# The forward substitution of the RWKV-7 units on VectorE in place of GpSimd

## The chip, the cores and the metric

One core of one Trainium2 chip runs the whole program. Its engines are called by the names of the profile: PE (TensorE, with PEld for its weight loads), DVE (VectorE), ACT (ScalarE), POOL (GpSimd) and SP (SyncE, which only issues transfers here). The metric is the device time in microseconds (us) of one execution; the kernel before has a median of 2439.64 us over 3 runs.

## The reference, cut to what matters

The block handles 2048 tokens of width 1024. A normed input goes through one combined projection; half of its columns feed a retention group (4 heads), half an RWKV-7 group (8 heads of 64). Then come the output projection, a router and a top-2 mixture of 32 experts, and a last norm. The change lies in the RWKV-7 recurrence:

```
def step(state, inp):
    r_t, k_t, v_t, w_t, a_t, b_t = inp
    sa = jnp.einsum('bhvk,bhk->bhv', state, a_t)
    state = state * w_t[:, :, None, :] + sa[..., None] * b_t[:, :, None, :] + v_t[..., None] * k_t[:, :, None, :]
    return state, jnp.einsum('bhvk,bhk->bhv', state, r_t)

_, y = lax.scan(step, jnp.zeros((B, H, N, N), jnp.float32), xs)
```

The kernel works in chunks of 64 tokens. Within a chunk the recurrence becomes a linear system with a unit triangular 64x64 matrix for each head and chunk, and its inverse is what the forward substitution helps to make.

## The kernel before, in words

**Stages.** The first stage (about 1350 us) makes the projections, the retention and the RWKV-7 recurrence in 4 groups (`g`) of 512 tokens; the second the output projection (its matmuls write tiles `acc` from `wo` and `mT`), the residual and the router; the third the experts. The second stage's first matmuls run already while the last units of the first stage are under way.

**Groups.** For a group, `rwkv_proj` and `ret_head` run the projection matmuls on PE, 128x512 each, into PSUM tiles `pj`: 3368 matmuls write `pj` in the program. Each half of a weight block is loaded into `wraw` (L242), split by ACT (L245) and DVE (L246) into a high and a low part in `whl` (3 buffers), and read by 12 matmuls.

**Units.** RWKV-7 works in 16 units (`u`) of 128 tokens. For a unit `rwkv_prep` builds scaled keys and receptances, multiplies them on PE (`pb`), masks the products into `pt` on DVE (L459; 2 buffers) and makes a transposed copy (L463 on PE). The 32x32 diagonal blocks go through DRAM (`nl_d`, L469) and come back as `ln` (L476), 32 systems on 128 partitions with 32 right sides. The substitution has 31 steps of two operations, each of which needs the one before it: a product of a column of `xl` with a row of `ln` into `tm` (L481), and the sum into `xl` (L483), on 128x8 to 128x76 elements. `xl` goes to DRAM (`xl_d`, L485) and comes back as `t1s` and `t2s` and into `inv` (L498 to L503). `ln`, `xl` and `tm` have one buffer each.

**After it.** `rwkv_inv` transposes `t1s` on PE (L506), copies it on DVE (L507) and joins the blocks into the 64x64 inverses. `rwkv_chain` runs the two chunks through the state `sbd`, which goes from unit to unit; it ends with the sums into `yt` (L555). `rwkv_fin` norms and writes the unit's output.

**What sets the order.** The instructions of the first two stages are put in an order by a scheduler with priorities (10000 ahead for prep, inversion and chain, 9000 for `rwkv_fin`, 2000 for the weight split). It fixes the order of every engine when the program is built. On the chip each engine takes its instructions in that order, and an instruction that waits holds up what stands behind it. The third stage has an order written by hand.

Of the kernel before, what the change touches and what calls it, by code (L numbers as in the profile page):

```python
# [14 lines left out]
ALU = mybir.AluOpType  # L15
# [113 lines left out]
def build(tc, A, out, dbg=None, phases=3):  # L129
    nc = tc.nc  # L130
    V, SC, GP, PE, SY = nc.vector, nc.scalar, nc.gpsimd, nc.tensor, nc.sync
# [51 lines left out]
    if True:  # L183
# [195 lines left out]
        def rwkv_prep(u):  # L379
# [93 lines left out]
            xl = rp.tile([128, 8, 32], F32, name="xl")  # L473
# [4 lines left out]
            for t in range(31):  # L478
                n, r = 31 - t, t // 4 + 1
                tv = tm[:, 0:r * n].rearrange("p (s n) -> p s n", n=n)  # L480
                GP.tensor_tensor(tv, xl[:, 0:r, t:t + 1].to_broadcast([128, r, n]),  # L481
                                ln[:, t:t + 1, t + 1:32].to_broadcast([128, r, n]), op=ALU.mult)
                GP.tensor_tensor(xl[:, 0:r, t + 1:32], xl[:, 0:r, t + 1:32], tv, op=ALU.add)  # L483
            for q in range(4):
                SY.dma_start(xl_d[u].rearrange("l (r q) t -> q l r t", q=4)[q], xl[q * 32:(q + 1) * 32])  # L485
            ST[u] = (ar, pt, bkt, uv, bon, wc, lg)
# [162 lines left out]
        for g in range(NG):  # L649
# [7 lines left out]
            for u in range(u0, u0 + 4):  # L657
                with tc.high_priority(offset=PRW):
                    rwkv_prep(u)
                with tc.high_priority(offset=PRC):  # L660
                    rwkv_inv(u)
                if u >= 2:
                    with tc.high_priority(offset=PRF):
                        rwkv_fin(u - 2)
                if u >= 1:
                    with tc.high_priority(offset=PRC):
                        rwkv_chain(u - 1)
# [22 lines left out]
    if True:  # L690
# [167 lines left out]
        t, PEND = 0, []  # L858
# [410 lines left out]
        for NB in FB:  # L1269
            ss = s2.tile([128, NB], F32, name=f"ssf{NB}")  # L1270
            HF = []
            for i in range(NB):
                t = t0 + i
# [6 lines left out]
            for i in range(NB):  # L1280
                t = t0 + i
# [52 lines left out]
```

## Time and profile before

| | |
|---|---|
| median of 3 runs (lowest, highest) | 2439.64 us (2436.16, 2443.72) |
| the profiled execution: its time, its span | 2436.82 us, 2435.1 us |
| PE / DVE / ACT / POOL busy over the span | 91% / 68% / 47% / 47% |
| mean granted TensorE clock, as a share of 2.4 GHz | 0.948 |
| L481 and L483 on POOL | 992 operations, 179.6 and 185.2 us busy |

The span runs from the first to the last instruction of the program; 1.7 us lie around it. "Busy" is the union of an engine's instructions; idle time "before" a group of instructions is put down to what ended it.

### The profile page before, as it was taken

How to read it: one execution, taken by the hardware profiler on the slowest of the kernel's cores; microseconds unless marked ns; L12 is line 12 of the kernel's file. 1: busy time of each engine (PE TensorE's matmuls, PEld its weight loads, DVE VectorE, ACT ScalarE, POOL GpSimd, SP SyncE). 2: the span in 40 equal slices, each digit the busy share in tenths (PEclk: the TensorE clock that was granted, in tenths of full speed). 3: DMA queues.
4: the chain of work that ended last, by engine and by line, in shares of the span. 5: the costliest groups of instructions: out<-in, count | busy, mean ns of one | idle time of the engine just before them, and what ended most of it. 6: DMA issues, size and time to landing. Idle time of an engine off the chain costs nothing. (4 is left out here: it accounts for less than half of the span.)

```text
span 2435.1 us, 36402 instructions
## 1 busy us (share of the span) xinstructions
PE 2212.5 (91%) x11816; PEld 1815.3 (75%) x11817; DVE 1647.5 (68%) x3498; ACT 1135.7 (47%) x1932; POOL 1154.7 (47%) x1530
## 2 busy tenths in 40 slices
PE   5999899998999988999779999699999999899991
PEld 4888778887778877888668888477777777677770
DVE  4477776888667776686765666655555556777775
ACT  4343433534334344343322222356666666577773
POOL 2035444453442475235553233445555555577770
PEclk9998999999999999999869999799999999999995
DMA  6643255433544335433343354468888888899998
GB/s 211 206 151 98 75 174 149 130 104 100 167 122 132 90 96 159 129 102 95 91 118 116 105 197 144 145 225 251 250 250 249 248 251 249 286 387 386 383 358 294
DMA packets 291298, 454.78 MB, mean 187 GB/s; under 512 B 93392, under 2 KB 164496, under 8 KB 291088
## 3 DMA queue, kind: packets, MB, share of 16 engines
q1 hardware_dynamic: 277136, 414.10, 51.1%
q0 software_dynamic: 13824, 37.80, 6.8%
q8 instruction: 94, 1.54, 0.3%
q14 instruction: 100, 0.82, 0.1%
q10 hardware_dynamic: 144, 0.52, 0.1%
HBM read 375.18 MB, written 81.85 MB: 188 GB/s over the span
## 5 line engine op out<-in xcount | busy, mean ns | idle before, releaser
L148 PE MATMUL pj<-nT,whl 128*128 128x512 f32 x2496 | 627.3, 403 | 12.4 <-DVE nT L315 5.3
L148 PEld LDWEIGHTS pj<-nT,whl 128*128 128x128 f32 x2496 | 465.8, 192 | 109.5 <-DVE nT L315 5.8
L148 PE MATMUL acc<-hl,xT 128*128 128x512 f32 (+1 forms) x2048 | 502.8, 400 | 1.7 <-DVE xT L169 1.4
L908 DVE TENSOR_TENSOR hl<-raw,hl 128x1024 fp32r<-128x1024 f32 x259 | 371.0, 1460 | 152.7 <-ACT hl L907 152.6
L908 POOL TENSOR_TENSOR hl<-raw,hl 128x1024 fp32r<-128x1024 f32 x125 | 337.4, 2709 | 252.0 <-ACT hl L907 235.4
L148 PEld LDWEIGHTS acc<-hl,xT 128*128 128x128 f32 (+1 forms) x2048 | 368.4, 182 | 105.5 <-DVE xT L169 1.5
L907 ACT CAST hl<-raw 128x1024 fp32r<-128x1024 f32 x353 | 360.3, 1048 | 75.0 <-DMA raw<-in_wu_dram 37.7
L245 ACT CAST whl<-wraw 128x512 fp32r<-128x512 f32 x248 | 152.5, 618 | 301.5 <-PE pj L148 233.0
L246 DVE TENSOR_TENSOR whl<-wraw,whl 128x512 fp32r<-128x512 f32 x248 | 185.2, 750 | 131.4 <-ACT whl L245 129.8
L148 PE MATMUL acc<-hl,hT 128*128 128x512 f32 (+1 forms) x1024 | 260.0, 404 | 1.0 <-DVEq L1221 1.0
L481 POOL TENSOR_TENSOR tm<-xl,ln 128x60 f32<-128x60 f32 (+24 forms) x496 | 179.6, 362 | 103.8 <-DMA ln<-nl_d 53.6
L148 PEld LDWEIGHTS acc<-hl,hT 128*128 128x128 f32 (+1 forms) x1024 | 183.2, 184 | 50.9 <-DVEq L1221 1.5
L483 POOL TENSOR_TENSOR xl<-xl,tm 128x60 f32<-128x60 f32 (+24 forms) x496 | 185.2, 373 | 36.5
L148 PE MATMUL acc<-wo,mT 128*128 128x512 f32 x768 | 191.6, 402 | 0.0
L148 PEld LDWEIGHTS acc<-wo,mT 128*128 128x128 f32 x768 | 143.1, 191 | 28.8
L494 POOL COPY mbd<-pt 32x128 f32<-32x128 f32 x64 | 20.1, 315 | 226.1 <-DVE pt L459 200.5
L1138 POOL DMA_INDIRECT h_d<-yo,ti x48 | 103.1, 2148 | 46.3 <-DMA h_d<-yo,ti 33.2
L148 PE MATMUL pj<-whl,nT 128*128 128x256 f32 x768 | 117.9, 305 | 0.3 <-ACT whl L245 0.3
L148 PEld LDWEIGHTS pj<-whl,nT 128*128 128x128 f32 x768 | 105.7, 207 | 2.7 <-ACT whl L245 0.5
L459 DVE TENSOR_TENSOR pt<-pb,cst 64x512 f32<-64x512 f32 x128 | 87.9, 687 | 18.6 <-PE pb L148 16.7
L169 DVE TENSOR_TENSOR xT<-tp,xT 128x512 fp32r<-128x512 f32 x80 | 53.7, 686 | 55.9 <-ACT xT L168 53.7
L148 PE MATMUL pb<-ar,bk 64*128 64x128 f32 x512 | 77.8, 299 | 4.6 <-DVE pt L459 3.3
(445 smaller groups left out, 3279.9 us busy)
## 6 DMA issues: line engine op xcount, KB each, us to landing
raw<-in_wg_dram SPq DMA_DIRECT2D x128, 512.0 KB, 4.9
raw<-in_wu_dram SPq DMA_DIRECT2D x128, 512.0 KB, 6.1
raw<-in_wd_dram SPq DMA_DIRECT2D x128, 512.0 KB, 6.5
wraw<-in_win_dram SPq DMA_DIRECT2D x208, 256.0 KB, 3.0
tr<-pf_d SPq DMA_DIRECT2D x80, 256.0 KB, 3.1
pf_d<-ev SPq DMA_DIRECT2D x52, 256.0 KB, 2.9
x<-in_xt_dram SPq DMA_DIRECT2D x32, 256.0 KB, 5.4
pf_d<-x SPq DMA_DIRECT2D x32, 256.0 KB, 4.0
```

Of the source, the lines that this page charges most:

```text
L148: PE.matmul(o, l, r, start=start, stop=stop)
L169: V.tensor_tensor(dst_l, ps, dst_h.bitcast(F32), op=ALU.subtract)
L245: SC.copy(hl[:, 0], raw)
L246: V.tensor_tensor(hl[:, 1], raw, hl[:, 0].bitcast(F32), op=ALU.subtract)
L459: V.tensor_tensor(pt[zs, i:i + 2, :, z ^ h], psp[zs].rearrange("p (f c) x -> p f c x", f=2), maskp[zs, None, None, :].to_broadcast([64, 2, ...
L481: GP.tensor_tensor(tv, xl[:, 0:r, t:t + 1].to_broadcast([128, r, n]), ln[:, t:t + 1, t + 1:32].to_broadcast([128, r, n]), op=ALU.mult)
L483: GP.tensor_tensor(xl[:, 0:r, t + 1:32], xl[:, 0:r, t + 1:32], tv, op=ALU.add)
L494: GP.tensor_copy(mbd[i * 32:(i + 1) * 32, :, i * 32:(i + 1) * 32], pt[i % 2 * 64:i % 2 * 64 + 32, :, i // 2, 0, 32:64])
L907: (SC.copy if hi is SC else hi.tensor_copy)(hl[:, 0], raw)
L908: lo.tensor_tensor(hl[:, 1], raw, hl[:, 0].bitcast(F32), op=ALU.subtract)
L1138: GP.indirect_dma_start(out=h_d, out_offset=bass.IndirectOffsetOnAxis(ap=idx, axis=0), in_=y, in_offset=None, bounds_check=S + 127, comput ...
```

## The change

The two operations of each step are issued to VectorE. Their operands, shapes, buffers and the transfers around them stay. Because the order of all engines is found anew for the changed program, instructions move on every engine in the first two stages; no instruction is added or taken away.

```
             for t in range(31):
                 n, r = 31 - t, t // 4 + 1
                 tv = tm[:, 0:r * n].rearrange("p (s n) -> p s n", n=n)
-                GP.tensor_tensor(tv, xl[:, 0:r, t:t + 1].to_broadcast([128, r, n]),
+                V.tensor_tensor(tv, xl[:, 0:r, t:t + 1].to_broadcast([128, r, n]),
                                 ln[:, t:t + 1, t + 1:32].to_broadcast([128, r, n]), op=ALU.mult)
-                GP.tensor_tensor(xl[:, 0:r, t + 1:32], xl[:, 0:r, t + 1:32], tv, op=ALU.add)
+                V.tensor_tensor(xl[:, 0:r, t + 1:32], xl[:, 0:r, t + 1:32], tv, op=ALU.add)
```

On DVE the first steps of unit 0 now stand as follows (a piece of the difference; `hv`, `rs_y` are a norm's statistics, `qT` and `ev` the rotary embedding of a retention head):

```order
 L413 RECIPROCAL inv_1163<-inv_1163 128x8
+L481 TENSOR_TENSOR tm<-xl,ln 128x31
 L372 TENSOR_REDUCE hv_2448<-pk 128x4
+L483 TENSOR_TENSOR xl<-xl,tm 128x31
 L373 TENSOR_SCALAR hv_2448<-hv_2448 128x4
-L154 TENSOR_SCALAR rs_y_2451<-hv_2448 128x4
+L481 TENSOR_TENSOR tm<-xl,ln 128x30
 L583 TENSOR_TENSOR qT<-pj,cs_t 128x512
 L584 TENSOR_TENSOR ev<-pj,sn_t 64x512
 L585 TENSOR_TENSOR ev<-pj,sn_t 64x512
+L483 TENSOR_TENSOR xl<-xl,tm 128x30
+L154 TENSOR_SCALAR rs_y_2451<-hv_2448 128x4
```

The steps are threaded between other work of DVE. Over the whole program 437 of the 992 stand directly behind another of them, 555 behind something else. From a unit's first L481 to its last L483 there stand 32 to 134 other DVE instructions, 1245 in all 16 units (80, 32, 47 and 73 in the last four).

On PE, this is what stood ahead of the transposition of `t1s` of unit 12 before (`psr`, `psz` are the chain of a unit, `pk` a retention head):

```order
L148 MATMUL pj<-whl,nT_9617 128x256 x3
L148 MATMUL pj<-whl,nT_9621 128x256 x3
L148 MATMUL pj<-whl,nT_9617 128x256 x3
L148 MATMUL pj<-whl,nT_9621 128x256
L148 MATMUL pb<-ar,bk 128x128 x4
L148 MATMUL pk<-qT,kT 128x128 x4
L148 MATMUL pj<-whl,nT_9621 128x256
L506 MATMUL psi<-cst,t1s 128x128
```

And this is what stands there now:

```order
L148 MATMUL pb<-tr,cst 128x512
L443 MATMUL pb<-cst,tr 128x128 x4
L148 MATMUL acc<-wo_12978,mT 128x512 x3
L148 MATMUL acc<-wo_12977,mT 128x512 x6
L148 MATMUL acc<-wo_12976,mT 128x512 x6
L148 MATMUL acc<-wo_12975,mT 128x512
L148 MATMUL psz<-uv,bkt 128x128 x4
L148 MATMUL psr<-uv,pt 64x64 x4
L148 MATMUL acc<-wo_12975,mT 128x512 x5
L148 MATMUL acc<-wo_12982,mT 128x512 x2
L506 MATMUL psi<-cst,t1s 128x128
```

The projections that stood there are all ahead of it now, and matmuls of the output projection have taken their place. Of the 3368 matmuls that write `pj`, 3065 stood ahead of unit 12's last L463 (the end of its prep on PE) and 3352 do now. Ahead of the L506 of unit 15 stood 247 matmuls of the output projection, and stand 312 now. Between the L506 of units 13 and 14 there is now neither a projection nor an output matmul:

```order
L506 MATMUL psi<-cst,t1s 128x128
L148 MATMUL psi<-t1s,mbd 128x32 x4
L148 MATMUL pb<-cst,tr 128x8 x4
L148 MATMUL psi<-t2s,wbd 128x32 x4
L417 MATMUL pb<-cst,tr 128x128 x4
L148 MATMUL psz<-rs__11287,inv_148 128x64 x4
L148 MATMUL psz<-uv,bkt 128x128 x4
L148 MATMUL psz<-uv,pt 64x64 x4
L566 MATMUL psi<-cst,yt 128x128 x4
L148 MATMUL psi<-lg,lw 128x128 x4
```

Of the units' own work nothing has gone from this piece: it is inversion, prep, chain and norm of neighbouring units.

## Rows read from the trace of the kernel before

**Rows 1.** The page's first part: busy time, share of the span, instructions.
```profile
PE 2212.5 (91%) x11816; PEld 1815.3 (75%) x11817; DVE 1647.5 (68%) x3498; ACT 1135.7 (47%) x1932; POOL 1154.7 (47%) x1530
```

**Rows 2.** Busy time by stretch: PE, PEld, DVE, ACT, POOL, clock, DMA.
```profile
167.00:1341.00 1174.00, 1081.47 (x6355) 919.31 (x6354) 846.53 (x1988) 446.52 (x928) 548.37 (x1206) 0.94 0.40 118
...
1560.00:2435.00 875.00, 795.39 (x3656) 611.99 (x3656) 566.88 (x687) 550.63 (x714) 508.65 (x222) 0.96 0.87 289
```

**Rows 3.** The page's groups: the substitution on POOL (count, busy us, mean ns, idle).
```profile
L481 POOL TENSOR_TENSOR tm<-xl,ln 128x60 f32<-128x60 f32 (+24 forms) x496 | 179.6, 362 | 103.8 <-DMA ln<-nl_d 53.6
...
L483 POOL TENSOR_TENSOR xl<-xl,tm 128x60 f32<-128x60 f32 (+24 forms) x496 | 185.2, 373 | 36.5
```

**Rows 4.** Timeline of POOL: first and last steps of units 12 and 15.
```profile
1098.57 0.24 POOL L481 TENSOR_TENSOR tm<-xl,ln 128x31 f32<-128x31 f32 x1
...
1132.31 0.21 POOL L483 TENSOR_TENSOR xl<-xl,tm 128x8 f32<-128x8 f32 x1
...
1315.56 0.24 POOL L481 TENSOR_TENSOR tm<-xl,ln 128x31 f32<-128x31 f32 x1 [6.25 <-DMA ln<-nl_d]
...
1341.01 0.21 POOL L483 TENSOR_TENSOR xl<-xl,tm 128x8 f32<-128x8 f32 x1
```

**Rows 5.** Waits of PE from 167 to 1341 us: us, times, longest.
```profile
PE psi L506 <- DMA t1s<-xl_d: 36.3, 14, 6.0
```

**Rows 6.** Groups by shape on DVE, 0 to 1600 us: small operations.
```profile
L829 DVE TENSOR_TENSOR oh<-oh,ps 128x64 f32<-128x64 f32 x12 | 2.1, 218 | 0.0
...
L804 DVE TENSOR_TENSOR ie<-lg,ge 128x64 f32<-128x64 f32 x6 | 1.5, 242 | 0.1
...
L829 DVE TENSOR_TENSOR oh<-oh,ps 128x32 f32<-128x32 f32 x8 | 1.3, 185 | 0.0
```

**Rows 7.** Timeline of DVE: small operations, independent and dependent.
```profile
1411.56 0.17 DVE L154 TENSOR_SCALAR rs_y<-sv 128x2 int32<-128x2 int32 x1
1411.64 0.16 DVE L156 TENSOR_SCALAR rs_h<-sv 128x2 f32<-128x2 f32 x1
1411.77 0.17 DVE L155 TENSOR_SCALAR rs_y<-rs_y 128x2 int32<-128x2 int32 x1
1411.97 0.16 DVE L158 TENSOR_TENSOR rs_t<-rs_y 128x2 f32<-128x2 f32 x1
1412.16 0.16 DVE L159 TENSOR_TENSOR rs_t<-rs_t,rs_h 128x2 f32<-128x2 f32 x1
```

**Rows 8.** The weight split L246 on DVE: the page's group; its shortest, median, longest.
```profile
L246 DVE TENSOR_TENSOR whl<-wraw,whl 128x512 fp32r<-128x512 f32 x248 | 185.2, 750 | 131.4 <-ACT whl L245 129.8
...
L246 DVE TENSOR_TENSOR whl<-wraw,whl x248: 660/693/1809, 25.6 to 1171.9; 128x512 fp32r<-128x512 f32 x124
```

**Rows 9.** The rotary operation on either engine, first 1400 us.
```profile
L586 POOL TENSOR_TENSOR qT<-qT,ev 128x512 f32<-128x512 f32 x16 | 25.0, 1560 | 24.4 <-DVE ev L585 19.9 <-DMA ev<-in_x_dram 4.5
...
L583 DVE TENSOR_TENSOR qT<-pj,cs_t 128x512 f32<-128x512 f32 x16 | 10.9, 684 | 1.6 <-PE pj L148 1.3
```

**Rows 10.** Waits of DVE from 167 to 1341 us, the longest two.
```profile
DVE whl L246 <- ACT whl L245: 81.2, 72, 3.1
DVE t1s L507 <- PE psi L506: 26.3, 9, 6.6
```

**Rows 11.** Busy time by stretch, as rows 2: DVE's busiest tenth; the units 12 to 15.
```profile
500.00:600.00 100.00, 91.33 (x573) 80.61 (x571) 82.02 (x180) 41.22 (x82) 43.74 (x82) 0.93 0.33 95
...
1099.00:1341.00 242.00, 211.96 (x1235) 182.50 (x1234) 161.54 (x419) 75.77 (x165) 119.45 (x286) 0.88 0.35 104
```

**Rows 12.** Timeline: the last mask of unit 12's prep, and its L506.
```profile
1091.20 0.69 DVE L459 TENSOR_TENSOR pt<-pb,cst 64x512 f32<-64x512 f32 x1
...
1139.58 0.30 PE L506 MATMUL psi<-cst,t1s 128*128 128x128 f32 x1 [2.22 <-DMA t1s<-xl_d]
```

**Rows 13.** Busy time of instructions on `pj`, then on `acc`: PE first, with count.
```profile
167.00:1341.00 1174.00, 647.45 (x2825) 490.44 (x2823) 111.40 (x194) 65.58 (x101) 0.94 0.40 118
...
1092.00:1341.00 249.00, 56.20 (x229) 42.05 (x230) 5.32 (x8) 0.00 (x0) 0.88 0.36 106
```

**Rows 14.** Waits of SP's queue from 167 to 1341 us.
```profile
SPq L485 <- POOL xl L483: 61.5, 11, 9.2
```

## The prediction

> **What bounds the kernel now.** I read the busy shares first [rows 1]: PE leads with 91%, DVE has 68% and POOL 47%. A share over the whole span says little, so the next view is busy time by stretch, cut where the first substitution begins (167 us) and the last one ends (1341 us) [rows 2]. Two things are to be seen there. In these 1174 us PE is busy 1081.47 us (92%) at a granted clock of 0.94, that is, partly on its lower level of 1.2 GHz; DVE is busy 846.53 us (72%) and idle 327. And the stretch from 1560 us on holds nothing that the change touches. So the question is whether the 1174 us grow or shrink, and DVE is the engine to watch.
>
> PE is not bound by its own work alone. The waits of PE name one line above all [rows 5]: the transposition L506 waits 36.3 us in 14 units for `t1s`, the result of the substitution on its way through DRAM. The substitutions lie on a loop: masks, transfer, substitution, transfer, inversion, chain. As `pt` has two buffers, the masks of a unit wait for the chain two units before. The four last units show its pace when little else is left: from the last mask of unit 12 at 1091.9 us [rows 12] to the end of the substitution of unit 15 at 1341.2 us [rows 4] it takes 249 us, 70 per unit from unit to unit behind the first one's 40.
>
> **The operations themselves.** POOL spends 179.6 + 185.2 = 364.8 us on them, 22.8 us per unit [rows 3]; from first to last step it takes 33.9 us in unit 12 and 25.7 us in unit 15 [rows 4], as other POOL work stands between. The trace has no such operation on DVE. The nearest rows are two-input operations from SBUF with 64 and 32 elements, 218 to 242 and 185 ns [rows 6]; the steps have 50 elements in the mean, so 0.21 us. How much DVE time one adds depends on its neighbours. Where an operation needs the one before it, the next starts 0.035 us after its end (L155 to L158 to L159: starts 0.20 and 0.19 apart, 0.16 to 0.17 long); where it doesn't, it starts 0.08 us before that end (L154 to L156) [rows 7]. So a step directly behind another costs 0.21 + 0.035 = 0.245 us, one between other work 0.21 - 0.08 = 0.13 us. By the counts in the section on the change that is 437 x 0.245 + 555 x 0.13 = 107 + 72 = 179 us; the bounds are all 992 at 0.13 and all at 0.245, 129 and 243 us. The Trainium skill (VectorE: DVE Perf Modes, section "The DRAIN you can't avoid") says that the next operation does not start until the pipeline has emptied; by it all steps would cost their full length, 208 us. The same section excepts operations that are not held, and the overlap in the trace says that the exception is the rule here, so I keep 179.
>
> Something is given back. A weight split takes 693 ns in the median but 750 in the mean and up to 1809 [rows 8], and I put the excess down to POOL working on the same memory at the time. That is 248 x 0.057 = 14 us; half as much again for DVE's other operations between SBUF tiles makes about 20. It is an estimate, with 0 and 30 as its bounds. DVE then has 846.5 + 179 - 20 = 1006 us to do where it had 846.5: 86% of the old 1174 us. Its busiest 100 us of before reach 82% [rows 11].
>
> **The substitution takes longer, not shorter.** Run alone, a unit's 62 steps would take 62 x 0.245 = 15.2 us on DVE. But they are threaded through DVE's other work: 1245 / 16 = 78 other instructions per substitution, worth 78 x 846.5/1988 = 33 us at the mean of the stretch [rows 2], plus 179/16 = 11 us of its own. That is 44 us with DVE never idle, against 26 to 34 on POOL in the units shown. In the last four units 58 others per substitution give 25 + 11 = 36 us against about 30. What stands behind a step in DVE's queue now also stands behind its first wait for `ln`; POOL waited 53.6 us for that in all [rows 3], and there nothing urgent stood behind it.
>
> **Where the time goes.** The order on PE shows the consequence: the units fall behind the projections. I take four terms.
>
> First, unit 12's prep ends later: 3352 - 3065 = 287 more projection matmuls stand ahead of its end. One costs 647.45 / 2825 = 0.229 us of PE [rows 13], together 66 us; at PE's busy share of 92% that is 71 us. Other matmuls moved past that point roughly cancel out (more retention, less inversion and chain).
>
> Second, the last four units. Then only 16 projection matmuls are left to fill PE instead of 303, so this stretch is paced by the loop. I let it take its 249 us as before, plus 8: each substitution is some 6 us longer, of which a third is won back where chain steps find PE and DVE free.
>
> Third, work done ahead: 312 - 247 = 65 more output matmuls are over when unit 15 is inverted, at 56.20 / 229 = 0.245 us each [rows 13]: -16 us.
>
> Fourth, waits up to unit 12. Some of the 36.3 us at L506 go, as more PE work now stands between masks and L506; I take half, -18. DVE at 86% delays other evictions and splits: of its 327 us of idle time only 81.2 are waits for the weight split [rows 10], which mostly follows PE; the rest are waits for results, which more work does not fill. I take +18, between nothing and the 54 us at which 1006 us of work would run at 82%.
>
> The sum is 71 + 8 - 16 + 0 = +63 us. The profiled execution took 2436.82 us, 1.7 more than its span and 2.8 under the median, so the forecast is 2436.8 + 63 = 2500 us. What the edit costs at SP is counted as nothing: the substitution issues no transfers, and SP's wait at `xl_d` (61.5 us [rows 14]) only changes its cause. It is covered by weight loads that are issued four buffers ahead; without that cover each 10 us more per substitution would hold up PE.
>
> **Rivals.**
>
> *The substitution gets faster and PE stops waiting.* POOL needs 1.56 us for a 128x512 rotary operation, DVE 0.68 for one of that size with an input in PSUM [rows 9], and 15 us alone is less than 22.8. If DVE ran the steps at this pace, the result would be there before PE asks. Then the 36.3 us [rows 5] go, and with them perhaps half of what the clock costs: 6% of 1081 us of PE [rows 2], 32 us. That is 2437 - 68 = 2369 us in full, and 2403 if half comes true. It decides if a substitution on DVE ends within about 35 us; the 33 us of other work threaded through it speak against that. Chance 0.13. The Trainium skill (GPSIMD Engine Reference, section "Engine selection") sends elementwise work to VectorE and calls GpSimd about twice as slow, which is this case; the trace agrees for 512 elements, while for 31 elements POOL's 0.24 us [rows 4] is near DVE's 0.185.
>
> *The loss is absorbed.* The last units could run through their loop faster because PE is free of projections: 178 us in place of 249, 46 per unit, would cancel the 71 us, and the time stays at about 2437. Against it: PE is busy 212 of 242 us there [rows 11], but its work can go only as fast as the chain of a unit lets it, and masks, inversion and chain all pass through DVE. Chance 0.08.
>
> *DVE becomes the bound.* If DVE keeps all its idle time of 327 us, its 160 us of net extra work lengthen the stretch one for one: 2437 + 160 = 2597, and 2437 + 243 = 2680 at the upper price with nothing given back. It decides if DVE's waits are for results that its own lateness delays. The share of waits that are not for the weight split speaks for it, PE's lead against it. Chance 0.17.
>
> **How the numbers follow.** My forecast has the remaining 0.62, with a range of its own of 2450 to 2560: the fourth term from -36 to +54, the first with 57 to 80 us. The range that should hold the time 8 times in 10 reaches from 2420, which leaves out the better half of the first rival, to 2600, which takes in the third one's middle. A measurement of this kernel can tell about 0.3% (7 us) from no change. Slower has 0.62 + 0.17 = 0.79, faster 0.13 and a little from the second rival, 0.14, same 0.07.
>
> **What would show it.** Right: on DVE, steps of about 0.21 us and some 44 us from first to last in the middle units; DVE busy about 1006 us between the first and the last step; the last L483 at about 1341 + 63 + 16 = 1420 us; PE idle in the last units, at a clock lower than 0.88; the stretch of the experts unchanged. Wrong: substitutions that end in 25 us, or waits at L506 near zero with the last L483 before 1341 us (first rival); a long row of PE waits for DVE in the middle of the stretch with DVE over 90% busy (third rival).

## The result, and the profile after

The changed kernel takes 2499.07 us in the median of 4 runs (2493.8 to 2500.97), the one before 2441.59 in 4: a ratio of 1.024, 95% interval 1.0216 to 1.0264, slower. The profiled execution has a span of 2496.9 us where before had 2435.1, 62 us more.

The first part of the page, in the columns of [rows 1]:

```profile
PE 2233.3 (89%) x11816; PEld 1831.5 (73%) x11817; DVE 1813.9 (73%) x4490; ACT 1138.9 (46%) x1932; POOL 795.5 (32%) x538
```

POOL gave up 359 us of busy time, DVE took on 166, and PE has the same work (its 21 us more go with a lower mean granted clock, 0.934 against 0.948). Shares alone would not tell why this is slower: no engine is near 100%. So I cut the span where the forecast cut it: at the first step of a substitution, at the end of unit 12's masks, at the last step of unit 15. Busy time by stretch, the changed kernel:

```profile
170.00:1159.00 989.00, 920.71 (x5393) 781.25 (x5391) 843.69 (x2368) 389.94 (x789) 165.00 (x178) 0.95 0.40 120
1159.00:1409.00 250.00, 197.67 (x1071) 168.41 (x1072) 178.83 (x642) 64.11 (x148) 26.49 (x40) 0.77 0.30 86
1409.00:2497.00 1088.00, 971.66 (x4661) 764.24 (x4659) 700.83 (x1292) 607.85 (x841) 582.18 (x291) 0.95 0.78 259
```

The same view of the kernel before:

```profile
167.00:1092.00 925.00, 862.51 (x5078) 730.79 (x5077) 679.67 (x1559) 368.72 (x760) 425.73 (x916) 0.95 0.41 121
1092.00:1341.00 249.00, 218.96 (x1278) 188.52 (x1277) 166.86 (x429) 77.80 (x169) 122.64 (x290) 0.88 0.36 106
1341.00:2435.00 1094.00, 990.88 (x4769) 780.23 (x4768) 709.60 (x1318) 612.62 (x851) 584.45 (x294) 0.95 0.78 259
```

By the cuts in time the 62 us appear in the first row: 989 us against 925, and in it PE is busy 58 us longer, with 315 more records of matmuls. PE was hardly kept waiting longer there (idle 68 us against 62); it was given other work first. In the second row PE is idle 52 of 250 us at a clock of 0.77, where it was 30 of 249 at 0.88 [rows 11]; the last four units now run with little beside them. The third row is 6 us shorter, with 108 fewer matmuls and 19 us less of PE's busy time.

Counted by PE, whose work is unchanged, the 62 us are 41 us more idle time and 21 us more busy time. Of the idle time 6 us lie up to unit 12, 22 in the last four units and 13 behind the last step. So the work done ahead is not itself lost; it is missing later, beside the last four units. The longest of PE's waits behind that step, one of 11.6 us for a unit's norm on POOL, has no counterpart in the kernel before, where L566 waits 1.4 us in all:

```profile
PE psi L566 <- POOL yt L375: 11.6, 1, 11.6
```

The groups of the substitution, which answer to [rows 3]:

```profile
L481 DVE TENSOR_TENSOR tm<-xl,ln 128x60 f32<-128x60 f32 (+24 forms) x496 | 118.4, 239 | 30.6 <-DMA ln<-nl_d 21.3
...
L483 DVE TENSOR_TENSOR xl<-xl,tm 128x60 f32<-128x60 f32 (+24 forms) x496 | 119.4, 241 | 8.9 <-DVE rs_t L159 0.3
```

The shortest, median and longest of L481, in ns:

```profile
L481 DVE TENSOR_TENSOR tm<-xl,ln x496: 148/213/1274, 170.1 to 1408.3; 128x60 f32<-128x60 f32 x16, 128x28 f32<-128x28 f32 x12, 128x66 f32<-128x66 f32 x11, 128x48 f32<-128x48 f32 x10
```

The operations became shorter, 0.24 us against 0.36 and 0.37; the substitutions became longer. The timeline of DVE while unit 15 is solved shows how:

```profile
1393.13 0.23 DVE L481 TENSOR_TENSOR tm<-xl,ln 128x72 f32<-128x72 f32 x1
1393.28 0.16 DVE L160 SCALAR_TENSOR_TENSOR rs_y<-rs_t,rs_y 128x2 f32<-128x2 f32 x1
1393.35 0.17 DVE L794 SCALAR_TENSOR_TENSOR ae<-ae,ct 128x16 f32<-128x16 f32 x1
1393.43 0.23 DVE L483 TENSOR_TENSOR xl<-xl,tm 128x72 f32<-128x72 f32 x1
1393.58 0.16 DVE L158 TENSOR_TENSOR rs_t<-rs_y 128x2 f32<-128x2 f32 x1
1393.65 0.17 DVE L796 TENSOR_REDUCE ai<-ae 128x2 f32<-128x16 f32 x1
1393.73 0.68 DVE L748 TENSOR_TENSOR w<-acc,w 128x512 f32<-128x512 f32 x1
1394.33 0.22 DVE L481 TENSOR_TENSOR tm<-xl,ln 128x68 f32<-128x68 f32 x1
```

From the sum at 1393.43 to the next product at 1394.33 pass 0.90 us, because an output tile's addition (L748, 0.68 us) stands between. From first to last step a substitution takes 46.3 us in the mean of the 16 units (31 to 74), where POOL took 32.3 (26 to 45). Nearly all of this is in units 0 to 11, 50.7 us against 32.7; the last four take 33.3 against 30.9.

The waits of PE at L506, which answer to [rows 5]:

```profile
PE psi L506 <- DMA t1s<-xl_d: 9.9, 7, 2.4
```

They have nearly gone, although the substitutions are longer.

### The profile page after: what moved, and what is told of

Read it like the earlier page. It is cut to its first block, busy times and chain, and to the rows that moved or that the text cites. A ratio compares the mean times of both kernels' runs of the same rounds, so it can differ in the third digit from the quotient of the medians.

```text
span 2496.9 us, 36385 instructions
## 1 busy us (share of the span) xinstructions
PE 2233.3 (89%) x11816; PEld 1831.5 (73%) x11817; DVE 1813.9 (73%) x4490; ACT 1138.9 (46%) x1932; POOL 795.5 (32%) x538
## 5 line engine op out<-in xcount | busy, mean ns | idle before, releaser
L246 DVE TENSOR_TENSOR whl<-wraw,whl 128x512 fp32r<-128x512 f32 x248 | 189.2, 766 | 93.2 <-ACT whl L245 91.9
L481 DVE TENSOR_TENSOR tm<-xl,ln 128x60 f32<-128x60 f32 (+24 forms) x496 | 118.4, 239 | 30.6 <-DMA ln<-nl_d 21.3
L483 DVE TENSOR_TENSOR xl<-xl,tm 128x60 f32<-128x60 f32 (+24 forms) x496 | 119.4, 241 | 8.9 <-DVE rs_t L159 0.3
L1138 POOL DMA_INDIRECT h_d<-yo,ti x48 | 104.2, 2171 | 45.6 <-DMA h_d<-yo,ti 32.3
L148 PE MATMUL pj<-whl,nT 128*128 128x256 f32 x768 | 107.8, 292 | 3.7 <-ACT whl L245 2.7
L148 PEld LDWEIGHTS pj<-whl,nT 128*128 128x128 f32 x768 | 98.0, 195 | 6.0 <-ACT whl L245 3.4
L148 PE MATMUL pb<-ar,bk 64*128 64x128 f32 x512 | 84.0, 312 | 11.1 <-DVE pt L459 9.3
L148 PEld LDWEIGHTS pb<-ar,bk 64*128 64x128 f32 x512 | 70.5, 212 | 25.2 <-issue 13.0
```

The source lines that it names most:

```text
L148: PE.matmul(o, l, r, start=start, stop=stop)
L246: V.tensor_tensor(hl[:, 1], raw, hl[:, 0].bitcast(F32), op=ALU.subtract)
L481: V.tensor_tensor(tv, xl[:, 0:r, t:t + 1].to_broadcast([128, r, n]), ln[:, t:t + 1, t + 1:32].to_broadcast([128, r, n]), op=ALU.mult)
L483: V.tensor_tensor(xl[:, 0:r, t + 1:32], xl[:, 0:r, t + 1:32], tv, op=ALU.add)
L1138: GP.indirect_dma_start(out=h_d, out_offset=bass.IndirectOffsetOnAxis(ap=idx, axis=0), in_=y, in_offset=None, bounds_check=S + 127, comput ...
```

## The experiments

The loop theory: each unit passes masks, substitution, inversion and chain in a loop, and a longer substitution makes the units fall behind the projections. Its rivals: the load theory (DVE's extra busy time costs, wherever it lies) and the tail theory (the last four units, without projections beside them, cost). The differences in us below are ratios times the time of before in the same session, 2434 to 2438 us; "the stretch up to unit 12" is the one of the first row above.

**e1_last4: units 12 to 15 alone on DVE.**

The edit, against the changed kernel:

```
+            E = V if u >= 12 else GP
...
-                V.tensor_tensor(tv, ...)
+                E.tensor_tensor(tv, ...)
...
-                V.tensor_tensor(xl[:, 0:r, t + 1:32], ...)
+                E.tensor_tensor(xl[:, 0:r, t + 1:32], ...)
```

> Only units 12 to 15 run their substitution on DVE, units 0 to 11 stay on GpSimd. Loop theory (the loss is the lag that units 0 to 11 gather against the projections because each substitution takes some 14 us longer; the last four units take as long as before): about the time before, -10 to +10 us. Tail theory (the loss arises in the last four units, where PE stands idle at its lower clock): most of the +57 us, +40 or more. Load theory (DVE's extra busy time costs, wherever it lies): a quarter, about +14 us.

Ratio 1.0107 (1.0077 to 1.0137), +26 us: no theory's number. Busy time by stretch, up to the masks of unit 12 and to the end of unit 15's substitution:

```profile
167.00:1089.00 922.00, 862.64 (x5078) 730.29 (x5077) 678.53 (x1560) 368.84 (x760) 426.84 (x916) 0.95 0.40 122
1089.00:1367.00 278.00, 237.78 (x1376) 202.13 (x1375) 213.64 (x702) 82.50 (x177) 36.52 (x44) 0.89 0.33 100
```

The first row is that of before, the second 29 us longer. In these four units the substitutions take 47, 62, 33 and 29 us, 43 in the mean where POOL took 31. So the last units are not free of charge: with projections still beside them, DVE has much to thread in.

**e2_first12: units 0 to 11 on DVE, the last four on POOL** (`u < 12` in the edit above).

> Units 0 to 11 on DVE, the last four on GpSimd. Loop theory: nearly the whole loss, +50 to +65 us. Tail theory: under +20 us. Load theory: three quarters, about +43 us.

Ratio 1.0138 (1.0072 to 1.0204), +34 us, by the profiled execution 30. Again it is no theory's number; it lies between those of the tail and the load theory. Its stretches:

```profile
170.00:1152.00 982.00, 911.12 (x5390) 772.95 (x5388) 843.45 (x2366) 389.42 (x788) 165.36 (x178) 0.96 0.40 120
1152.00:1376.00 224.00, 181.81 (x968) 154.08 (x969) 132.87 (x368) 61.28 (x142) 104.43 (x285) 0.78 0.32 91
```

Up to unit 12 the whole lag is there (982 against 925). Then 25 us are won back: with few projections left beside them, the late units run through the loop in 224 us instead of 249. Their substitutions take 27.3 us in the mean on POOL, 33.3 on DVE in the changed kernel, where the same late units take 250 us. That the changed kernel needs as long as before there is therefore two things that cancel, 25 us won by an emptier PE and 26 lost by the substitution on DVE. By the pair of e1 and e2, the last four units account for 24 to 26 us and the first twelve for about 34.

**e3_pool_twice: POOL, every product made twice.** DVE gets nothing.

```
-                GP.tensor_tensor(tv, ..., op=ALU.mult)
+                for _ in range(2):
+                    GP.tensor_tensor(tv, ..., op=ALU.mult)
```

> The substitution stays on GpSimd, but each product is made twice (the same values again), 93 operations in place of 62 per unit: 11 us longer per substitution, with no work added to DVE. Loop theory: slower by much of what the change costs, +30 to +60 us, and the order again puts more projections ahead of a unit's prep. Load theory: no change, within 10 us.

Ratio 1.0309 (1.0243 to 1.0375), +75 us. The substitutions take 45.9 us in the mean, as long as in the changed kernel, and the order puts the same 3352 projection matmuls ahead of the end of unit 12's prep:

```profile
168.00:1170.00 1002.00, 917.69 (x5410) 775.70 (x5409) 706.20 (x1619) 386.82 (x787) 568.61 (x1297) 0.96 0.38 117
1170.00:1420.00 250.00, 183.75 (x961) 156.35 (x962) 137.23 (x375) 63.68 (x144) 142.09 (x407) 0.73 0.30 87
```

PE's busy time up to unit 12 (918 us against 921), the 250 us behind it and the low clock there are those of the changed kernel, without a microsecond of load moved to DVE. So a longer substitution is enough without any load on DVE, and the load theory, which expected no change, falls as the only cause. One rival is not excluded here: POOL has 143 us more to do up to unit 12 (569 against 426), and its other results come later too. PE waits 13.6 us for L375's `rc` in place of 5.4. What of the 75 us that makes was not taken apart.

**e4_dve_load: POOL as before, 992 more operations on DVE that nobody reads.**

```
+            dx = rp.tile([128, 8, 32], F32, name="dx")
...
+            V.memset(dx, 0.0)
...
+                V.tensor_tensor(dv, dx[..., t:t + 1] ..., cst[..., t + 1:32] ..., op=ALU.mult)
+                V.tensor_tensor(dx[..., t + 1:32], dx[..., t + 1:32], dv, op=ALU.add)
```

> The substitution stays on GpSimd; DVE gets 62 more operations of the same shapes per unit on tiles of their own (zeros times a constant), which nobody reads. DVE is then as busy as in the changed kernel and more, GpSimd as in the one before. Load theory: +50 us or more, as the change. Loop theory: under +25 us, only what masks, copies and evictions are delayed by behind the extra operations.

Ratio 1.0194 (1.0128 to 1.0259), +47 us. The substitutions stay at 33.0 us and the order hardly moves (3077 projection matmuls ahead of unit 12's prep, 3065 before), so here the loop theory's bound falls. Its stretch up to unit 12:

```profile
177.00:1147.00 970.00, 875.86 (x5075) 739.28 (x5074) 798.66 (x2248) 370.21 (x759) 435.63 (x916) 0.93 0.38 116
```

With the same count of matmuls as before PE needs 13 us more busy time, at a clock of 0.93, and is idle 94 us instead of 62. The last four units stay as they were (246 us, PE idle 34 against 30). About 10 of the 47 us lie ahead of the first step, which starts at 177 us in place of 167, because some of the added operations stand there (DVE is busy 151 us up to that step, 91 before); in the changed kernel it starts at 170.

**e5_load_low: the same load at the priority of the projections.** The added lines of e4 stand ahead of `ret_head` in the loop over heads.

> The substitution stays on GpSimd; DVE gets the same 992 extra operations as in e4_dve_load, on tiles of their own, but issued with the retention heads at the priority of the projections, so that they fill gaps and do not stand ahead of a unit's masks and copies on purpose. If DVE's extra busy time itself costs (load theory): +45 to +55 us, as e4_dve_load. If it cost there because it held up the steps of the loop (loop theory in its wider form): under +20 us.

Ratio 1.0146 (1.0106 to 1.0186), +36 us. Neither number came out. Up to unit 12:

```profile
176.00:1135.00 959.00, 875.27 (x5059) 738.09 (x5058) 804.97 (x2241) 367.69 (x755) 430.36 (x916) 0.94 0.39 117
```

Three quarters of e4's cost stay when the operations are not urgent, which speaks for DVE's time itself; but the intervals of the two runs overlap, and here too 9 us lie ahead of the first step.

**e7_dve_fused: the changed kernel with product and sum of the first 8 steps in one operation.**

```
+                if t < 8:
+                    for s in range(r):
+                        V.scalar_tensor_tensor(xl[:, s, t + 1:32], ln[:, t, t + 1:32], xl[:, s, t:t + 1],
+                                               xl[:, s, t + 1:32], op0=ALU.mult, op1=ALU.add)
+                    continue
```

> The changed kernel, but the first 8 steps make product and sum in one operation (scalar_tensor_tensor, one for each right side): 58 operations per unit in place of 62, and 54 of them in a chain. The order puts 3268 projection matmuls ahead of the end of unit 12's prep, 84 fewer than in the changed kernel. Loop theory: 84 x 0.229 / 0.92 = 21 us less than the changed kernel, so +30 to +45 us against before. Load theory: four operations fewer in 62 give 4 us at most, +50 to +57.

Ratio 1.0098 (1.006 to 1.0135), +24 us: 33 less than the changed kernel, on the side of the loop theory and beyond its figure. The substitution takes 41.4 us in the mean.

**e8_pool_half and e9_dve_half: the last 15 of the 31 steps left out, on POOL and on DVE.** The inverses are incomplete in both.

```
-            for t in range(31):
+            for t in range(16):
```

> GpSimd as before, but the last 15 of the 31 steps are left out (the inverses are then incomplete): 32 operations per unit, some 11 us less per substitution. If the loop still paces the kernel before: -30 us or more. If PE's own work paces it as soon as the substitution is no longer late: between 0 and -30 us, by the waits at L506 that go.

> The changed kernel with the last 15 of the 31 steps left out (incomplete inverses): 32 operations per unit on DVE, half of the extra load, and a substitution of about 24 us, shorter than on GpSimd before. Its order has the units as early as before (3077 projection matmuls ahead of unit 12's end of prep, 3065 before). Loop theory: within -25 to +10 us of before. Load theory: half of the loss of e4_dve_load, +25 us.

POOL: ratio 0.9895 (0.9846 to 0.9944), -26 us. DVE: 0.9811 (0.9775 to 0.9847), -46 us. At half the length the exchange of engines gains some 20 us (13 between the profiled executions), although DVE's substitution still takes longer (27.2 us in the mean against 17.4). The waits of PE at L506, first of e8, then of e9:

```profile
PE psi L506 <- DMA t1s<-xl_d: 26.1, 14, 4.2
```

```profile
PE psi L506 <- DMA t1s<-xl_d: 8.3, 8, 2.4
```

These waits go with the engine, not with the length. With every substitution on POOL they are 26 to 42 us (36 before, 41 in e3, 42 in e4, 28 in e5, 26 in e8), whether it takes 17 or 46 us; with it on DVE they are 5 to 14 (10 changed, 14 in e7, 8 in e9, 5 in e12). A likely reason, not tested, is the order: it leaves PE too little to do before L506 when POOL makes the result, and about enough when DVE does. But these waits are not what e9 gains on e8: PE's idle time over the span is 198 us in both, as other waits take their place, and the 13 us are PE's busy time (2204.6 against 2191.3 us).

**e10, e11, e12: three tries at a better version.** e10 takes e7's fused steps for units 0 to 11 and POOL for the last four. e11 is the kernel before with its first four steps on DVE, one operation each:

```
+                if t < 4:
+                    V.scalar_tensor_tensor(xl[:, 0, t + 1:32], ln[:, t, t + 1:32], xl[:, 0, t:t + 1],
+                                           xl[:, 0, t + 1:32], op0=ALU.mult, op1=ALU.add)
+                    continue
```

e12 is e7 with its last 24 columns solved in blocks of 4 (`l4` are the rows of `ln` by blocks, joined within their 4x4 diagonal blocks by 12 operations beside the first 8 steps):

```
+            for b in range(2, 8):
+                n, r, c = 31 - 4 * b, b + 1, 4 * b
...
+                V.tensor_tensor(pv, xl[:, 0:r, None, c:c + 4] ..., l4[:, b, :, c + 1:32] ..., op=ALU.mult)
+                V.tensor_reduce(tv, pv, axis=AX.X, op=ALU.add)
+                V.tensor_tensor(xl[:, 0:r, c + 1:32], xl[:, 0:r, c + 1:32], tv, op=ALU.add)
```

> Units 0 to 11 as in e7_dve_fused (DVE, the first 8 steps in one operation each), units 12 to 15 on GpSimd as before. e2_first12 was 29 us faster than the changed kernel by the same exchange in the last four units. If the two effects add: +24 - 29, that is -15 to +5 us against before. If the last four units only gained in e2 because they came late: as e7_dve_fused, +15 to +25 us.

> GpSimd as before, but the first 4 steps (one right side, 31 to 28 elements) are made on DVE, each in one operation: 58 operations per unit, 54 of them on GpSimd, and one more change of engine per unit. Loop theory: GpSimd's part is 2 to 3 us shorter per substitution, -15 to 0 us. If a change of engine costs as much as it saves, or DVE's head waits for ln: 0 to +10 us.

> On DVE, with fewer and wider operations: the first 8 steps as in e7_dve_fused; for the last 24 columns the rows of each 4x4 diagonal block are first joined (12 operations of 192 elements, beside those 8 steps), then each block of 4 columns takes a product, a sum over 4 and an addition. 42 operations per unit, 30 of them in a chain, but wider, about the same busy time as the changed kernel. If the number of dependent steps is what counts, between which other work is threaded: below e7_dve_fused, 0 to +15 us against before. If the busy time on DVE counts: +25 us or more. The order puts 3272 projection matmuls ahead of unit 12's end of prep, as many as in e7_dve_fused (3268), which speaks for about +24.

e10: ratio 1.0038 (1.0012 to 1.0063), +9 us; the two effects add to about half, 15 us less than e7 where 29 were hoped for. e11: 1.0064 (1.0044 to 1.0084), +16 us; its waits at L506 grew to 51.0 us. The steps saved on POOL shorten nothing: from first to last step it takes 32.3 us in the mean, as before. e12: 1.0156 (1.0116 to 1.0196), +38 us, with 42 operations and a substitution of 38.6 us in the mean, shorter than e7's. Its measured time is above e7's all the same, though the intervals overlap (1.0116 to 1.0196 against 1.006 to 1.0135). By its own expectation this is the side of DVE's busy time, which is 18 us more than in e7 over the first 1600 us. The order puts as many projections ahead as in e7. So neither that count nor the length of the substitution orders these versions alone. No version with all its steps beats the kernel before.

## Why the prediction was right

The forecast was 2500 us, +63; the profiled span grew by 62. The mechanism held: DVE's other work stretches the substitution, the units fall behind the projections, and the last four run with little beside them. That the sum fits within 1 us is partly luck: its terms missed by 4, 7 and 10 us, and the misses cancel. Point by point:

**The price of a step** was right: behind another step the next starts 0.034 us after its end (0.035 forecast), behind other work 0.077 us before that end (0.08), and the median is 0.213 us (0.21). The mean of 0.240 was not foreseen: 41 steps took over 0.35 us, and each of them began while a POOL operation was under way and ended just after it. DVE's busy time in the stretch is 1022.5 us, forecast 1006.

**"Something is given back" was wrong.** The weight split L246 has a mean of 766 ns after, 750 before [rows 8]; the excess did not go with POOL's steps, because it was not theirs. Before, 88 splits met only small POOL operations, nearly all of them steps, and took 714 ns in the mean against 689 alone: 2 us in all. Of the 15 us of excess 12.5 lay in 15 splits of over 0.9 us, and each of these had begun while a 512-wide two-input operation of POOL was under way. The change leaves those operations in place, and after it there are 20 such splits. One of them, with the operation that it met:

```profile
412.36 1.31 POOL L586 TENSOR_TENSOR qT<-qT,ev 128x512 f32<-128x512 f32 x1 [4.05 <-DVE ev L585]
412.44 1.78 DVE L246 TENSOR_TENSOR whl<-wraw,whl 128x512 fp32r<-128x512 f32 x1
```

The split ends at 414.22 us, 0.55 us behind the end of POOL's operation. All 35 long splits of the two kernels end 0.546 to 0.554 us behind such an end. So the two engines do hinder each other, but by turns: the operation that comes second waits.

**The longer substitution** was right: 46.3 us against 44 forecast, in the last four units 33.3 against 36. e3 shows that such a length moves the units as far behind without load on DVE. **The first term** came out at +67 us (masks of unit 12 at 1159 us instead of 1092, forecast 71), with 58 us of it PE's busy time, 6 its idle time and 3 a later start. **The second** gave +1 us (250 against 249, forecast +8), but its parts were mis-sized: e2 shows 25 us won by an emptier PE, a third of the 71 us that the rival "the loss is absorbed" asks for, and the substitution on DVE takes as much back. By these two terms the last L483 ends at 1408.6 us, where 1420 was named. **The third** was mis-sized, -6 us for -16: the work done ahead took 19 us off PE's busy time behind the last step, but its idle time grew by 13, with a wait of 11.6 us at L566 among it, to which the forecast gave no term. **The fourth**, a guess of zero, lies within the 67 us and came out near it: PE's idle time up to unit 12 is 68 us against 62, with 26 us of waits at L506 gone over the whole stretch and others, mostly for DVE's and ACT's results, in their place.

The rival that the waits at L506 go was right about the waits and wrong about the time. The rival that DVE becomes the bound did not come true: DVE is busy 83% of the stretch, 85% up to unit 12, and PE's share of idle time there stays at 7%. But e4 and e5 show that the load has a price of its own, 36 to 47 us, where POOL keeps the substitution. How much of it is in the changed kernel is not shown. By place its loss does not look like e4's: up to unit 12 PE's idle time is 6 us longer than before, 32 in e4 and 21 in e5; in the last four units it is 22 longer, 36 in e3 and 4 in e4. These effects do not add: 75 us for the length on POOL and 36 to 47 for the load stand against 57 for both with the exchange of engines. How the 57 us divide is not settled, nor why e12 is not faster than e7. A third buffer for `pt`, which would have tested the loop directly, was not tried.

## What to carry to other kernels

Moving a chain of small dependent operations to an engine with shorter instructions need not shorten the chain if that engine has other work to thread in: count what the order puts between two steps before comparing the price of one. Where a scheduler fixes the order, read from the new order what has moved ahead of what, and price that with rows of the old trace; here the count of projection matmuls ahead of unit 12 gave the first term within 4 us. The count does not tell everything: in e4 it stayed, and the kernel lost 47 us. Work that is done ahead is no loss by itself; ask what the engine will have to do where that work is then missing. A stretch that takes "as long as before" can hide a gain and a loss of the same size; exchange one part alone to see both.

## What the runs showed of the hardware that was not expected

Less overlap in time between DVE and POOL did not make DVE's operations shorter in the mean: the weight split went from 750 to 766 ns while POOL's busy time between the first and the last step fell from 548 to 191 us. What counts is which POOL operation is met, and who comes first. In the two kernels 39 splits (two inputs from tiles in SBUF) began while POOL was in a two-input operation on 512 elements with over 0.2 us of it left. Of these 37 took 0.78 to 1.82 us and ended 0.55 us after POOL's operation; in the other two POOL's operation ended last. Over all 13 runs, each of the 213 splits of over 0.9 us ended so. Three splits that began beside a fill (L445, L446) with 0.25 to 0.38 us of it left took their usual 0.69 us. A split that met small operations of POOL alone, most of them substitution steps, took 25 ns more in the mean.
